# Raw weight blocks behind the mixers on GpSimd's queue, and the residual factors of up behind its third block

## The chip, the cores and the metric

The kernel runs on one core of a Trainium2 chip. The metric is device time in microseconds (us) of one execution. The core's engines work side by side, each through its own instruction list in order: TensorE (PE, with its weight loads as PEld), VectorE (DVE), ScalarE (ACT), GpSimd (POOL) and SyncE (SP). Data moves between memory and the core by transfers that an engine issues into its queue; an instruction that waits for a semaphore holds up everything behind it on that engine.

## The reference

One inference step of a decoder layer, for 512 prompt tokens and 8 decode tokens (520 columns), width 2048, in float32:

```python
y, new = mixer(rmsnorm(x, w['g_mix']), ...)        # RG-LRU and mLSTM heads, w_in and w_out
x = x + y
x = x + cross_attn(rmsnorm(x, w['g_xattn']), mk, mv, w)   # w_mk, w_mv, w_cq, w_co, 4 heads, 256 memory tokens
hf = rmsnorm(x, w['g_ffn'])
x = x + jnp.square(jax.nn.relu(hf @ w['w_up'])) @ w['w_down']   # 2048 -> 8192 -> 2048
```

A final norm follows. `w_mk`, `w_out`, `w_cq`, `w_mv` and `w_co` are 2048 x 2048 each, `w_up` and `w_down` four times that.

## The kernel before, in words

The first 600 us project the input (`w_in`) and run the mixers. Everything after that, "behind the mixers", is built by `rest()` as one list of jobs: half of the keys (`w_mk`), the output projection ("out"), the other half of the keys, the queries ("cq"), the values (`w_mv`) with the attention between them, "co", "up" with 32 units, and four groups of "down" (`d0` to `d3`) with 8 units each.

A large product is done by a Strassen-like scheme (`strassen`): a unit is a 2 x 2 arrangement of weight blocks, made into seven products of 24 matmuls each; in the middle of up a unit takes about 20 us. Each float32 matrix is split into a rounded part and a rest. For a weight block ScalarE casts the rounded part `whi` and VectorE subtracts to get `wlo` (`split_weights`, L98), so each block costs a cast of 1.05 us and a subtraction of 1.22 us. Some of the seven products need sums of raw blocks, made by VectorE at L821.

Raw weight blocks of 512 KB are fetched by `fetch` (L869), the line in question is L876. They land in seven rotating buffers (`raw`, sums too are `raws`), or, at the joints between down groups, in a stage buffer (`rawp`). `load` issues on SP's queue and `store` on GpSimd's; both are the same kind of transfer. Fetches stand some four to seven products ahead of their use and a load must wait until its buffer was read for the last time.

The other operand is a set of seven precomputed operand blocks (`op`), spilled to memory by `spill` (L832, on GpSimd: `tdup`, `tdd0` to `tdd3`, ...) and read back by `batch_load` (L845, on SP), then cast by ScalarE (L846) and subtracted by VectorE (L841). The last block of a set goes from the chip directly (`set_tail`, L861). For the keys, `mem_load` (L1143) reads four operand tiles `op<-dmem`; the first time it does so on GpSimd.

A scheduler with a cost model orders the instructions of each engine behind the mixers, with priorities for fetches and evacuations. The order on an engine is fixed when the kernel is built.

`scale_back` is a task that steps along with the jobs. It forms two factors (inverses by Ln and Exp on ScalarE, each with a table load, L1292 and L1293, and VectorE steps L1294, L1295, L1306, L1309), then reads eight residual blocks (`x<-dx`, L1315), multiplies them (L1319) and stores them on GpSimd (L1320), for use as the starting values of down (`down_load`, L1339). Before, it is started when up begins and lets 16 steps go by first. In up, `up_evac` (L1322) squares the output of a unit (L1329, L1330) and spills it. Down stores its sums by L1347 on GpSimd.

Of the kernel before, what the change touches and what calls it, by code (L numbers as in the profile page):

```python
# [11 lines left out]
AF = mybir.ActivationFunctionType  # L12
# [5 lines left out]
P = 128  # L18
TP = 512
NB = 8  # L20
T = TP + NB
# [24 lines left out]
def tile_trunk(ctx: ExitStack, tc: tile.TileContext, a, o):  # L46
    nc = tc.nc
    V, S, PE, G = nc.vector, nc.scalar, nc.tensor, nc.gpsimd
# [16 lines left out]
    def nm(s):  # L65
        uid[0] += 1
        return f"{s}_{uid[0]}"
# [22 lines left out]
    load = nc.sync.dma_start  # L90
    store = G.dma_start
# [26 lines left out]
    def start(gen, rate=None):  # L118

        tasks.append([gen, rate, 0.0])  # L120
# [152 lines left out]
    scl = keep.tile([P, T], F32, name="scl")  # L273
# [12 lines left out]
    st = {}  # L286
# [498 lines left out]
    def rest():  # L785
# [12 lines left out]
        def enter(name, **pools):  # L798
            def go():
                if "stack" in stage:  # L800
                    stage["stack"].close()
                stage.clear()
                stage["stack"] = ExitStack()
                for n, bufs in pools.items():
                    stage[n] = pool(name + n, bufs, stage["stack"])
            return go

        def tl(tag, shape, dt=F32):
            return stage[tag].tile(list(shape), dt, tag=tag, name=nm(tag))
# [13 lines left out]
        def mixed(b, t):  # L823

            sub(b[:, 0:2], t[:, 1:3], t[:, 0:2])
            sub(b[:, 2], t[:, 2], b[:, 0])
            sub(b[:, 3], t[:, 3], b[:, 2])

        def spill(key, k, wa, wb=None):
            d = td[key][k // 4][:, :, k % 4]  # L830
            if wb is None:
                store(d, wa)  # L832
            else:
                store(d[:, 0:4], wa)
                store(d[:, 4:8], wb)
# [29 lines left out]
        seq, sources, raws, ws = [], [], {}, {}  # L865
# [3 lines left out]
        def fetch(k, q):  # L869
            if k not in seconds:  # L870
                t = praw.tile([P, 8, P], F32, tag="raw", name=nm("raw"))
            else:
                n = "y" if "y" in stage else "x"
                t = stage[n].tile([P, YROW] if n == "y" else [P, 2 * T], F32, tag=n, name=nm("rawp"))
                t = t[:, 0:1024].rearrange("p (a b) -> p a b", b=P)
            load(t, sources[k][q])  # L876
            raws[k, q] = t

        def prep(n):
# [71 lines left out]
        def blocks(box, p):  # L951

            if p == 0:
                box["t"] = tl("t", (P, 4, HT))
            t, out = box["t"], box["out"]
            i = (0, 2, 1, 0, 2, 1, 3)[p]
            if p in (3, 4, 5):
                V.tensor_tensor(out=t[:, i], in0=out, in1=t[:, i], op=ALU.add)
            else:
                S.copy(t[:, i], out)  # L960
            return t
# [53 lines left out]
        def mean_of(v):  # L1015
            for c, ps in zip(HALF, st["ps"]):
                V.scalar_tensor_tensor(out=v[:, c], in0=ps, scalar=1.0 / D, in1=esc[:, c],
                                       op0=ALU.mult, op1=ALU.add)
# [63 lines left out]
        def attn_decode(h):  # L1082
# [23 lines left out]

            q = rows_split(512, dqd[h], None)
            cur = [fetch(b, a["K"]) for b in range(2)]
            for b in range(NB):
                yield  # L1110
                kt, qb = cur.pop(0), spread(q, b, 512)
                for i in range(2):
                    t = kt[:, i * 512:(i + 1) * 512]
                    V.tensor_tensor_reduce(out=t, in0=t, in1=qb, op0=ALU.mult, op1=ALU.add,
                                           scale=1.0, scalar=0.0, accum_out=sc[:, i, b:b + 1])
                if b + 2 < NB:
                    cur.append(fetch(b + 2, a["K"]))
            cur = [fetch(b, a["V"]) for b in range(2)]
            for _ in range(2):
                yield  # L1120
# [46 lines left out]
        def mv_job(h, g, w):  # L1167
            if g == 0:
                st["mv"] = [pacc.tile([P, 512], F32, tag="acc" + b, name=nm("mv")) for b in "bc"]
            wh, wl = (flat(t).rearrange("p (a b) -> p a b", a=2) for t in w)  # L1170
            for j in range(2):
                k = 2 * g + j
                xh, xl = mact[k]
                for i in range(2):
                    ms = slice(i * P, (i + 1) * P)
                    for wi, (x, u) in enumerate(((xh, wh), (xh, wl), (xl, wh))):
                        PE.matmul(st["mv"][i], x[:, ms], u[:, j], start=(k == 0 and wi == 0),  # L1177
                                  stop=(k == KB - 1 and wi == 2))
# [3 lines left out]
        def mv_post(h, g):  # L1182
            if g == 7:
                while h > 1 and not pv_done[h - 2]:
                    step_tasks()
                t = tl("kv", (P, 4 * HT))[:, 0:1024].rearrange("p (a b) -> p a b", a=2)
                for i in range(2):
                    S.activation(t[:, i], st["mv"][i], AF.Copy, scale=rmc[:, i:i + 1])
                    load(o["mv"][h, i], t[:, i])
                mvx[h] = hi, lo = op_tile((P, 2, 512)), op_tile((P, 2, 512))  # L1190
                S.copy(hi, t)
                lo_of(lo, t, hi)
# [92 lines left out]

        def up_enter():
            enter("d", x=2, r=1, t=2, w=2)()
            start(scale_back())

        def negative_inverse(y, t, v):  # L1290

            S.activation(y, v, AF.Ln)  # L1292
            S.activation(y, y, AF.Exp, scale=-1.0)  # L1293
            V.tensor_tensor(out=t, in0=v, in1=y, op=ALU.mult)  # L1294
            V.scalar_tensor_tensor(out=y, in0=t, scalar=2.0, in1=y, op0=ALU.subtract, op1=ALU.mult)  # L1295

        def scale_back():
            for _ in range(16):
                yield

            va, vb = tl("x", (P, 2, T)), tl("x", (P, 2, T))
            v, y, t = va[:, 0], va[:, 1], vb[:, 0]
            mean_of(v)
            st["rphi"] = tl("r", (P, T))
            negative_inverse(y, t, scl)
            V.scalar_tensor_tensor(out=st["rphi"], in0=y, scalar=-1.0, in1=v, op0=ALU.mult, op1=ALU.mult)  # L1306
            yield
            negative_inverse(y, t, v)
            V.scalar_tensor_tensor(out=scl, in0=y, scalar=-1.0, in1=scl, op0=ALU.mult, op1=ALU.mult)  # L1309
            yield  # L1310
            for u in range(KB // 2):
                for _ in range(6):
                    yield
                x = tl("x", (P, 2, T))
                load(x, dx[2][u])  # L1315
                for _ in range(6):
                    yield
                for i in range(2):
                    V.tensor_tensor(out=x[:, i], in0=x[:, i], in1=st["rphi"], op=ALU.mult)  # L1319
                store(dx[3][u], x)  # L1320

        def up_evac(u, p, box):  # L1322
            t = blocks(box, p)
            if u == UP - 1 and p == 0:
                box["w"] = tl("w", (P, 8, HT))
                enter("e", y=4, x=4)()
            if p == 6:
                w = box.pop("w", None) or tl("w", (P, 8, HT))
                S.activation(t, t, AF.Relu)  # L1329
                S.activation(w[:, 0:4], t, AF.Square)  # L1330
                mixed(w[:, 4:8], w[:, 0:4])
                spill(f"d{u // 8}", u % 8, w)

# [94 lines left out]
        for h in range(4):  # L1428
            plain([a["w_mv"][h, g] for g in range(8)],
                  lambda g, w, h=h: mv_job(h, g, w), lambda g, h=h: mv_post(h, g))  # L1430
        seq[first]["enter"] = att_enter
        seq[-1]["after"] = att_left
        strassen("co", 8, sq_src("w_co"), enter_=enter("c", x=2, w=2, sq=1, ss=1),
                 **residual(1, 2, C_FFN, "up"))
        strassen("up", UP, sq_src("w_up"), up_evac, up_enter, lambda s: set_load("d0", s),
                 hooks={(UP - 1, 3): lambda: (down_load(0), down_load(1))})

# [94 lines left out]
def _pack(i):  # L1532
# [58 lines left out]
    y=(KB, P, T), p_m=(4, 1), s_m=(4, NB), scv=(P, 2, 16, NB), cv=(16, P, 11), rh=(8, P, 9),  # L1591
# [39 lines left out]
```

## Time and profile before

| what | value |
| --- | --- |
| runs of the kernel | 2802.77 us median of 3 (2799.02 to 2803.41) |
| profiled execution | 2807.62 us, span 2805.8 us |
| mean granted TensorE clock | 0.977 |
| TensorE busy | 2689.8 us, 21122 matmuls |
| VectorE busy | 2263.9 us |
| ScalarE busy | 1389.2 us |
| GpSimd busy | 106.9 us |
| moved by transfers | 551.23 MB |

A row of a timeline gives the start from the span's begin, the length, the engine, the source line, the operation, output and inputs, the count, and in brackets the idle time before it with what ended that. A row of waits gives total, times and longest in us. Issues of transfers count for SP's queue as SPq, where the time of a row may hold its wait. A row of transfers gives count, size and median us from issue to landing. The profiled execution is 4.85 us above the median of the runs.

### The profile page before, as it was taken

What the parts mean: (1) busy time and instruction counts of PE and PEld (TensorE: products, weight loads), DVE (VectorE), ACT (ScalarE), POOL (GpSimd) and SP (SyncE); (2) the same over time, 40 slices, a digit from 0 to 9 for tenths busy, and PEclk for the clock granted to TensorE, in tenths of its full rate; (3) what the DMA queues carried; (4) which work ended last, traced back from release to release, by engine and by line L of the source; (5) the groups of instructions that cost most, each with busy time, mean ns of one, the idle gap of its engine ahead of it and who ended that gap; (6) DMA issues with size and microseconds to landing.
All of it is one profiled execution on the core that took longest, in us unless ns stands there. A gap on an engine that the chain in (4) does not pass through costs nothing.

```text
span 2805.8 us, 52010 instructions
## 1 busy us (share of the span) xinstructions
PE 2689.8 (96%) x21122; PEld 2612.2 (93%) x21122; DVE 2263.9 (81%) x3453; ACT 1389.2 (50%) x1857; POOL 106.9 (4%) x162
## 2 busy tenths in 40 slices
PE   7999999999999999989979999999999999999996
PEld 7999999999999997669969999999998999999996
DVE  7777787758888888889888777777788787988886
ACT  5455556525455445455464545554554353544543
POOL 0000000030000000000000000000000000000000
PEclk9999999999999999999989999999999999999998
DMA  4666642378677458885657454545457465564632
GB/s 168 191 214 212 198 144 90 104 273 272 217 247 270 158 188 296 314 328 179 220 198 255 148 170 145 173 144 172 146 191 277 146 237 180 207 209 153 234 110 80
DMA packets 178855, 551.23 MB, mean 196 GB/s; under 512 B 23724, under 2 KB 33644, under 8 KB 178616
## 3 DMA queue, kind: packets, MB, share of 16 engines
q1 hardware_dynamic: 153384, 455.28, 48.8%
q0 software_dynamic: 24080, 90.50, 8.9%
q8 instruction: 166, 2.72, 0.4%
q10 hardware_dynamic: 1152, 2.13, 0.2%
q14 instruction: 73, 0.60, 0.1%
HBM read 427.45 MB, written 120.51 MB: 195 GB/s over the span
## 4 chain that ended last, share of the span: by engine, by line
PE 80%; DMA 8%; DVE 6%; ACT 3%; issue 2%; SPq 0%; DVEq 0%; ACTq 0%
PE acca L942 33%; PE accc L942 16%; PE mm L166 12%; PE accb L942 9%; PE mv L1177 3%; PE mk L1157 2%; DVE wlo L102 1%; PE ax L185 1%; DMA op<-tdd 1%; PE row L1104 1%; DVE op L841 1%; PE aux L185 1%; ACT whi L101 1%; DMA ct<-in_C 1%; ACT op L846 1%
## 5 line engine op out<-in xcount | busy, mean ns | idle before, releaser
L942 PE MATMUL acca<-op,whi 128*128 128x260 f32 x5632 | 1042.8, 285 | 30.7 <-ACT t L960 11.9
L942 PEld LDWEIGHTS acca<-op,whi 128*128 128x128 f32 x5632 | 877.6, 190 | 35.6 <-ACT t L960 12.9
L942 PE MATMUL acca<-op,wlo 128*128 128x260 f32 x2816 | 802.7, 285 | 4.3 <-DVE wlo L102 4.2
L101 ACT CAST whi<-raw 128x1024 fp32r<-128x1024 f32 x388 | 406.8, 1050 | 441.9 <-PE acca L942 142.7
L942 PEld LDWEIGHTS acca<-op,wlo 128*128 128x128 f32 x2816 | 536.2, 190 | 6.3 <-DVE wlo L102 6.3
L102 DVE TENSOR_TENSOR wlo<-raw,whi 128x1024 fp32r<-128x1024 f32 x388 | 473.0, 1220 | 64.6 <-ACT whi L101 61.0
L942 PE MATMUL accc<-op,whi 128*128 128x260 f32 x2816 | 515.3, 282 | 1.4 <-DVE op L841 0.9
L101 ACT CAST whi<-raws 128x1024 fp32r<-128x1024 f32 x264 | 277.0, 1049 | 385.8 <-PE accc L942 111.5
L166 PE MATMUL mm<-xa,whi 128*128 128x260 f32 x2624 | 432.9, 287 | 14.2 <-ACT whi L101 8.9
L942 PEld LDWEIGHTS accc<-op,whi 128*128 128x128 f32 x2816 | 434.6, 188 | 3.8 <-issue 1.5
L102 DVE TENSOR_TENSOR wlo<-raws,whi 128x1024 fp32r<-128x1024 f32 x264 | 322.7, 1222 | 119.7 <-ACT whi L101 119.0
L942 PE MATMUL accc<-op,wlo 128*128 128x260 f32 x1408 | 397.2, 282 | 0.0
L166 PEld LDWEIGHTS mm<-xa,whi 128*128 128x128 f32 x2624 | 366.5, 191 | 16.1 <-ACT whi L101 8.9
L166 PE MATMUL mm<-xa,wlo 128*128 128x260 f32 x1312 | 268.8, 286 | 0.0
L942 PE MATMUL accb<-op,whi 128*128 128x260 f32 x1408 | 260.8, 285 | 8.1 <-ACT op L846 4.6
L942 PEld LDWEIGHTS accc<-op,wlo 128*128 128x128 f32 x1408 | 265.3, 188 | 0.0
L942 PEld LDWEIGHTS accb<-op,whi 128*128 128x128 f32 x1408 | 218.9, 190 | 9.5 <-ACT op L846 4.8
L166 PEld LDWEIGHTS mm<-xa,wlo 128*128 128x128 f32 x1312 | 204.2, 190 | 0.5 <-DVE wlo L102 0.3
L942 PE MATMUL accb<-op,wlo 128*128 128x260 f32 x704 | 199.3, 283 | 0.0
L841 DVE TENSOR_TENSOR op<-op,op 128x1040 fp32r<-128x1040 f32 (+3 forms) x136 | 159.9, 1179 | 37.6 <-ACT op L846 26.7
L846 ACT CAST op<-op 128x1040 fp32r<-128x1040 f32 (+1 forms) x112 | 112.2, 1006 | 96.6 <-DMA op<-tdd 51.3
L101 ACT CAST whi<-wraw 128x1024 fp32r<-128x1024 f32 x82 | 85.6, 1044 | 140.3 <-PE mm L166 116.7
(374 smaller groups left out, 3313.1 us busy)
## 6 DMA issues: line engine op xcount, KB each, us to landing
raw<-in_w_up SPq DMA_DIRECT2D x128, 512.0 KB, 3.4
raw<-in_w_down SPq DMA_DIRECT2D x100, 512.0 KB, 3.9
wraw<-in_w_in SPq DMA_DIRECT2D x80, 512.0 KB, 4.1
tdd<-w POOLq DMA_DIRECT2D x32, 1040.0 KB, 6.3
x<-dx SPq DMA_DIRECT2D x56, 520.0 KB, 4.8
op<-tdd SPq DMA_DIRECT2D x56, 520.0 KB, 6.7
dx<-x POOLq DMA_DIRECT2D x48, 520.0 KB, 4.8
raw<-in_w_mk SPq DMA_DIRECT2D x32, 512.0 KB, 5.6
```

The source lines that it names most:

```text
L101: S.copy(hi, raw)
L102: V.tensor_tensor(out=lo, in0=raw, in1=hi.bitcast(F32), op=ALU.subtract)
L166: PE.matmul(ps[:, hf, 0:HT], w[:, j, :], x[:, HALF[hf]], start=(k == 0 and wi == 0), stop=(k == n - 1 and wi == 2))
L185: PE.matmul(out, u, v, start=first and i == 0, stop=last and i == 2)
L841: V.tensor_tensor(out=lo, in0=src, in1=hi.bitcast(F32), op=ALU.subtract)
L846: S.copy(hi[:, 0:n], lo[:, 0:n].bitcast(F32))
L942: PE.matmul(out, u[:, k], x[:, j], start=(new and k == 0 and i == 0), stop=(k == 7 and i == 2), skip_group_check=not new)
L1104: PE.matmul(ps, identr[0:NB, b:b + 1].to_broadcast([NB, P]), r, start=i == 0, stop=i == 1)
L1157: PE.matmul(st["mk"], u[:, i, :], x, start=(k == 0 and wi == 0), stop=(k == KB - 1 and wi == 2))
L1177: PE.matmul(st["mv"][i], x[:, ms], u[:, j], start=(k == 0 and wi == 0), stop=(k == KB - 1 and wi == 2))
```

## The change

Every raw weight block behind the mixers is issued on GpSimd's queue instead of SP's: 416 loads of 512 KB (32 each for `w_mk`, `w_out`, `w_cq`, `w_mv`, `w_co`, 128 each for up and down). `scale_back` is started in the evacuation of unit 2 of up, its first Ln is ordered behind the Square of that evacuation (`mark`), and the mean is taken after the first inverse.

```diff
@@ fetch
-            load(t, sources[k][q])
+            store(t, sources[k][q])
@@ up_enter
-            start(scale_back())
@@ scale_back
-            for _ in range(16):
-                yield
...
-            mean_of(v)
             st["rphi"] = tl("r", (P, T))
-            negative_inverse(y, t, scl)
+            with tc.issue_after(st["mark"].ins):
+                negative_inverse(y, t, scl)
+            mean_of(v)
...
@@ up_evac
-                S.activation(w[:, 0:4], t, AF.Square)
+                ins = S.activation(w[:, 0:4], t, AF.Square)
+                if u == 2:
+                    st["mark"] = ins
+                    start(scale_back())
```

Since the scheduler works on the whole list, some instructions of VectorE and ScalarE change places too, most by a few rows.

GpSimd's list at the begin of the keys. Names are tile and source with running numbers; `tdout` rows are spills of the mixers' output. Before:

```order
L733 DMA tdout_1_114<-hh_489_3210 128x260
L734 DMA tdout_1_114<-kv_1017_7204 128x2x260
L1143 DMA op_1030_7482<-dmem_161 128x1024
L1143 DMA op_1032_7487<-dmem_161 128x1024
L1143 DMA op_1034_7492<-dmem_161 128x1024
L1143 DMA op_1036_7497<-dmem_161 128x1024
L982 DMA dx1_0_137<-x_1142_8142 128x1040
```

After:

```order
L734 DMA tdout_1_114<-kv_1017_7204 128x2x260
...
L876 DMA raw_1073_7632<-in_w_mk 128x1024
L876 DMA raw_1077_7663<-in_w_mk 128x1024
L876 DMA raw_1081_7697<-in_w_mk 128x1024
L876 DMA raw_1085_7728<-in_w_mk 128x1024
L1143 DMA op_1030_7482<-dmem_161 128x1024
L1143 DMA op_1032_7487<-dmem_161 128x1024
L1143 DMA op_1034_7492<-dmem_161 128x1024
L1143 DMA op_1036_7497<-dmem_161 128x1024
L876 DMA raw_1089_7762<-in_w_mk 128x1024
```

Ten raw loads now stand between the last spill and the four operand loads of the keys; the eighth to the tenth wait for the buffers of the first to the third.

SP's list where up begins, with raw loads among the reads of up's operand sets. Before:

```order
L845 DMA op_2293_16296<-tdup_1_120 128x780
L876 DMA raw_2331_16546<-in_w_up 128x1024
L845 DMA op_2299_16334<-tdup_0_119 128x1040
L845 DMA op_2301_16339<-tdup_1_120 128x780
L876 DMA raw_2337_16607<-in_w_up 128x1024
L845 DMA op_2305_16373<-tdup_0_119 128x1040
L845 DMA op_2307_16378<-tdup_1_120 128x780
L845 DMA op_2311_16412<-tdup_0_119 128x1040
L876 DMA raw_2349_16736<-in_w_up 128x1024
L845 DMA op_2313_16417<-tdup_1_120 128x780
L845 DMA op_2320_16464<-tdup_0_119 128x1040
L845 DMA op_2322_16469<-tdup_1_120 128x780
```

After:

```order
L845 DMA op_2293_16296<-tdup_1_120 128x780
L845 DMA op_2299_16334<-tdup_0_119 128x1040
L845 DMA op_2301_16339<-tdup_1_120 128x780
L845 DMA op_2305_16373<-tdup_0_119 128x1040
L845 DMA op_2307_16378<-tdup_1_120 128x780
L845 DMA op_2311_16412<-tdup_0_119 128x1040
L845 DMA op_2313_16417<-tdup_1_120 128x780
L845 DMA op_2320_16464<-tdup_0_119 128x1040
L845 DMA op_2322_16469<-tdup_1_120 128x780
```

The three raw loads are gone from between them, and the operand loads follow each other directly.

GpSimd's list at the end of the third down group, where the fourth takes its first blocks through stage buffers. After (before, these `raw` and `rawp` loads were on SP, `rawp_3740` right behind the last operand loads of that group's successor):

```order
L1348 DMA dx3_5_158<-x_3664_28620 128x1040
L876 DMA raw_3743_29270<-in_w_down 128x1024
L876 DMA raw_3744_29272<-in_w_down 128x1024
L876 DMA raw_3765_29420<-in_w_down 128x1024
L1348 DMA dx3_6_159<-x_3689_28846 128x1040
L1348 DMA dx3_7_160<-x_3690_28848 128x1040
L876 DMA rawp_3740_29238<-in_w_down 128x1024
L876 DMA rawp_3751_29314<-in_w_down 128x1024
```

`rawp_3740` now stands behind the last two residual stores of the group.

More of the change, by code (lines that the diff above doesn't have):

```diff
@@ L1297, in scale_back @@
         def scale_back():
-            for _ in range(16):
-                yield
             va, vb = tl("x", (P, 2, T)), tl("x", (P, 2, T))
             v, y, t = va[:, 0], va[:, 1], vb[:, 0]
+            st["rphi"] = tl("r", (P, T))
+            with tc.issue_after(st["mark"].ins):
+                negative_inverse(y, t, scl)
             mean_of(v)
-            st["rphi"] = tl("r", (P, T))
-            negative_inverse(y, t, scl)
             V.scalar_tensor_tensor(out=st["rphi"], in0=y, scalar=-1.0, in1=v, op0=ALU.mult, op1=ALU.mult)
```

## The prediction

> **What bounds the kernel now.** I read the page's busy times and queue shares first, then the windows by stage, then what SP's queue waits for, and last the timelines at the places where TensorE stands still.
>
> ```profile
> span 2805.8 us, 52010 instructions
> PE 2689.8 (96%) x21122; PEld 2612.2 (93%) x21122; DVE 2263.9 (81%) x3453; ACT 1389.2 (50%) x1857; POOL 106.9 (4%) x162
> ...
> q1 hardware_dynamic: 153384, 455.28, 48.8%
> q0 software_dynamic: 24080, 90.50, 8.9%
> ```
>
> TensorE is busy for 96% of the span, so at most 2805.8 - 2689.8 = 116 us could be had from any cover or reordering. The queue rows give time per byte: GpSimd's queue (software_dynamic) took 0.089 x 16 x 2805.8 / 90.50 = 44 us of one DMA engine per MB, SP's 0.488 x 16 x 2805.8 / 455.28 = 48. A byte is no dearer from GpSimd's queue.
>
> The windows by stage show where the idle time lies (columns: window, length, busy PE, PEld, DVE, ACT, POOL with counts, granted TensorE clock, DMA share, GB/s):
>
> ```profile
> 615.00:630.00 15.00, 10.88 (x74) 10.59 (x74) 10.05 (x13) 7.13 (x8) 0.00 (x0) 0.77 0.86 317
> 1254.00:1270.00 16.00, 7.32 (x39) 5.87 (x38) 15.73 (x22) 12.06 (x25) 0.00 (x0) 0.85 0.68 264
> 1427.00:1466.00 39.00, 19.48 (x116) 18.27 (x117) 34.37 (x44) 26.82 (x37) 0.56 (x1) 0.74 0.55 205
> 1600.00:2080.00 480.00, 480.00 (x4001) 480.00 (x4001) 371.90 (x405) 247.41 (x311) 20.34 (x24) 1.00 0.48 157
> ```
>
> In the middle of up TensorE never stops: nothing can be gained there, only lost. The change decides at stage entries: keys (615), co (1254), co to up (1427), and the four down groups.
>
> **The change, part one: 416 raw loads from SP's queue to GpSimd's.**
>
> ```profile
> SPq L876 <- DVE raws L821: 541.8, 103, 11.9
> SPq L876 <- DVE wlo L102: 353.1, 140, 12.7
> ...
> raw<-in_w_up SPq DMA_DIRECT2D x128, 512.0 KB, 3.4
> ...
> dx<-x POOLq DMA_DIRECT2D x48, 520.0 KB, 4.8
> ...
> L832 POOL DMA_DIRECT2D tdd<-w x32 | 27.2, 850 | 582.1 <-DVE w L821 501.6 <-ACT whi L101 36.7 <-DVE wlo L102 19.9
> L1143 POOL DMA_DIRECT2D op<-dmem x4 | 2.2, 546 | 15.3 <-DMA tdout<-hh 13.5 <-PE mm L166 1.8
> ```
>
> L876 is the raw load: SP stands for hundreds of us at it, until VectorE frees one of seven buffers. It issues in order, so an operand load (L845) behind it stands too. That is the cost the move can take away. Its own cost: one issue of 512 KB on GpSimd took 546 ns (L1143), so 416 x 0.546 = 227 us on an engine busy for 107 us: hidden. Landing goes from 3.4 us towards 4.8 (520 KB stores); the steady stage covers that:
>
> ```profile
> 1685.53 6.64 SPq L876 DMA_DIRECT2D raw<-in_w_up  x2
> 1693.32 1.23 DVE L821 TENSOR_TENSOR raws<-raw,raw 128x1024 f32<-128x1024 f32 x1
> ```
>
> The load issued at 1685.53 has its first use at 1693.32, the tightest of a unit: 7.8 us against 4.8. Queued behind it is a second raw load and then the spill `tdd<-w`; in the new order of GpSimd the raws stand in the sequence in which these were issued in time, so none waits for a later one. Steady units: 0.
>
> VectorE could be slowed by GpSimd's issues, or GpSimd by VectorE. The 0.85 us above are means over 32 issues made while VectorE was 77% busy (371.90 of 480), so 227 us more of such issues cost nothing visible; bounds 0 to a few us. The Trainium skill (SBUF — State Buffer, section SBUF: two separate sides) says that GpSimd cannot write descriptors while VectorE runs an operation that takes both ports, and advises loads on SP or ACT instead, against this change. The trace shows no such delay at 850 and 546 ns; by its figure of some 3.1 us for such a DMA instead of 0.62, an estimate from that page, each raw load would be 2.5 us later, still inside the 7.8.
>
> **Where it loses: the keys.** Four operand loads `op<-dmem` (L1143) already sit on GpSimd. In the new order ten raw loads stand ahead of them, the tenth waiting for VectorE's third `wlo`:
>
> ```profile
> 597.25 0.57 POOL L1143 DMA_DIRECT2D op<-dmem  x1
> 615.62 1.22 DVE L102 TENSOR_TENSOR wlo<-raw,whi 128x1024 fp32r<-128x1024 f32 x1
> 615.96 1.03 ACT L1144 CAST op<-op 128x1024 fp32r<-128x1024 f32 x1
> 617.04 0.79 PE L1157 MATMUL mk<-op,whi 128*128 128x256 f32 x2 [2.41 <-ACT op L1144]
> 619.91 0.58 PE L1157 MATMUL mk<-op,whi 128*128 128x256 f32 x1 [2.08 <-DVE op L841]
> ...
> op<-dmem POOLq DMA_DIRECT2D x4, 512.0 KB, 7.6
> ```
>
> That `wlo` ends at 616.84; the tenth raw load issues, then the four: first at 617.4. Landing 7.6 gives 625.0, the cast 1.03 more: TensorE begins at about 626 instead of 617.04. The second stall (2.08) then falls inside the first, so the loss is 9 - 2 = 7. The key jobs are bound by TensorE and make none of it up; later waits of the same stage (some 2 us before the next product) absorb a part. I take +5; bounds +2 (landing of 4.8) and +10 (nothing absorbed).
>
> **Where it gains: co to up.**
>
> ```profile
> 1445.83 0.33 SPq L876 DMA_DIRECT2D raw<-in_w_up  x1
> 1455.59 0.33 SPq L876 DMA_DIRECT2D raw<-in_w_up  x1
> 1456.01 1.33 SPq L845 DMA_DIRECT2D op<-tdup  x3
> 1465.18 0.96 DVE L841 TENSOR_TENSOR op<-op,op 128x780 fp32r<-128x780 f32 x1
> 1445.04 0.58 PE L942 MATMUL accb<-op,whi 128*128 128x260 f32 x1 [4.59 <-ACT op L846]
> 1463.34 0.80 PE L942 MATMUL acca<-op,whi 128*128 128x260 f32 x2 [10.05 <-ACT t L960]
> 1475.78 0.51 PE L942 MATMUL acca<-op,whi 128*128 128x260 f32 x2 [1.61 <-DVE t L958]
> ```
>
> SP stands at a raw load until 1445.83 and at the next until 1455.59, and the last three operand loads go at once behind it, at 1456, with nothing else in the trace that held them. TensorE loses 4.59 + 10.05 + 1.61 = 16.3 us. What is late next is VectorE: of the 39 us to 1466 it was busy for 34.4, so at most 4.6 us of idle close up in its part, and the moved residual work (below), three VectorE steps of 0.7, takes 2.1 us out of the stretch. The last `lo` ends 6.7 us earlier. The 1.61 at 1475.78 and the clock (0.74 in this window, since it follows the stalls) give a little more. I take -10; bounds -4 (VectorE's idle time alone) and -16 (all of TensorE's three waits).
>
> The same mechanism is smaller elsewhere. At the entry of co VectorE was busy for 15.73 of 16 us, so -1.5 (0 to -3). At the down groups:
>
> ```profile
> 2292.93 0.32 SPq L1339 DMA_DIRECT2D x<-dx  x1
> 2293.34 0.38 SPq L845 DMA_DIRECT2D op<-tdd  x1
> 2299.88 0.80 PE L942 MATMUL acca<-op,whi 128*128 128x260 f32 x2 [3.18 <-ACT whi L101]
> 2131.37 0.51 PE L942 MATMUL acca<-op,whi 128*128 128x260 f32 x2 [1.37 <-ACT whi L101]
> 2608.85 9.80 SPq L876 DMA_DIRECT2D rawp<-in_w_down  x3
> 2615.10 0.53 POOL L1347 DMA_DIRECT2D dx<-x  x1 [2.26 <-DVE x L949]
> 2619.45 0.39 PE L942 MATMUL acca<-op,wlo 128*128 128x260 f32 x1 [1.75 <-DVE wlo L102]
> ```
>
> At 2293 an operand load stood behind a residual load; in the new order it stands ahead of it, and the 3.18 goes: -4 with the slow clock after it (0 to -4). At the first group, 2131, the load behind residuals and raws came late: -2 (0 to -3). At the last group it turns round: the first `rawp` (a raw load into another buffer), issued at 2608.85 on SP, now stands behind both last residual stores of the group, so after 2615.6, 6.8 us later, and its cast, at 2614.7 before, moves to about 2620: +3 (0 to +5).
>
> **Part two: the residual factors.**
>
> ```profile
> 1436.57 1.28 ACT L1292 ACT_TABLE_LOAD   x1
> 1437.87 0.64 ACT L1292 ACTIVATE x<-scl 128x520 f32<-128x520 f32 x1
> 1468.24 0.70 DVE L1294 TENSOR_TENSOR x<-x 128x520 f32<-128x520 f32 x1 [2.09 <-ACT x L1293]
> ```
>
> Four table loads of 1.28 and four activations of 0.64, 7.7 us of ACT, leave co to up for units 2 and 3 of up, with five VectorE steps and sixteen multiplies of about 0.7. ACT is half busy there; VectorE has 0.23 x 20.2 = 4.6 us idle in each unit and the work is spread over seven units: 15 of 32 us. New in it: raws that stand on GpSimd behind residual stores, which wait for multiplies and for `x<-dx` loads. +1 (0 to +4). The gain of leaving was counted above.
>
> **Sum.** +5 - 10 - 1.5 - 4 - 2 + 3 + 1 = -8.5 us on the profiled execution's 2807.6 (span 2805.8 and 1.8 around it), 2799.1. The median of the runs, 2802.8, lies 4.8 below that execution, so the forecast is 2794.3. The ends of the terms add to -24 (2 - 16 - 3 - 4 - 3) and +15 (10 - 4 + 5 + 4), which all together are unlikely.
>
> **Rivals.** *No measurable change:* VectorE gives only its lower bound at co to up (-4), and the keys lose 8: +8 - 4 - 1.5 - 4 - 2 + 3 + 1 = +0.5, 2803. For it: VectorE at 88% in that window; TensorE needs its sets in order, and the last sets wait for VectorE. The Trainium skill (DMA: Bandwidth & Descriptors, Issuing engines are not separate DMA queues) says that issuing from several engines saves only the sequencer's time to issue. By that rule the 0.33 us of an SP issue is all there is to save, off the path, and the time would be about this rival's; the waits of 542 and 353 us in SP's queue speak against it, since these are waits of a queue and not bandwidth.
>
> *Larger gain:* the loads in advance let TensorE run through co to up (-16) while the keys lose only 2 and the last group nothing: 2 - 16 - 1.5 - 4 - 2 + 0 + 0 = -21.5, 2781.
>
> *Slower, through the tight raw load of every unit:* if a load on GpSimd's queue lands more than 7.8 us after its turn, each of 64 units of up and down waits for the excess. The four `op<-dmem` took 7.6, in a stretch with the DMA engines 86% busy; the stores of 520 KB took 4.8, and the steady stage has them 48% busy, so it is near the point only at the entries. At 1 us of excess: +64 - 8.5 = +55, 2858.
>
> **How the numbers follow.** Runs of this kernel agree to about 0.2% (5.6 us). My forecast case 0.5, no change 0.23, larger gain 0.14, slower units 0.08, the rest (a wider loss at keys, a reordering of VectorE that costs) 0.05. The forecast case spreads from 2786 to 2800: 0.40 of it faster, 0.10 same. No change: 0.17 same, 0.03 each way. With the larger gain's 0.14, faster is 0.57, same 0.27, slower 0.03 + 0.08 + 0.05 = 0.16. The range goes from 2781 to 2809: the larger gain, no change, and a small loss.
>
> **What would show it.** Right: the keys' first matmul near 626; operand loads of up on SP in one run without a raw between, all issued by 1440; the 10 us wait at 1463 gone, and the first unit of up ending near 1464; the wait at 2299.9 gone; steady units at the same length. Wrong: GpSimd's raw loads landing after 7 us in the middle of up, TensorE waits for `whi` or `raws` there, or VectorE operations longer than 1.22 us.

## The result, and the profile after

The changed kernel took 2819.86 us (median of 4 runs, 2817.94 to 2821.23) against 2802.11 for the kernel before: ratio 1.0055, 95% interval 1.0039 to 1.0072. It is slower by some 17.7 us; the forecast was 2794.3 with a range to 2809. The profiled execution has a span of 2819.4 us. Its page:

```profile
span 2819.4 us, 52063 instructions
PE 2689.6 (95%) x21122; PEld 2610.0 (93%) x21122; DVE 2261.6 (80%) x3453; ACT 1387.8 (49%) x1857; POOL 330.5 (12%) x578
...
q0 software_dynamic: 83984, 308.63, 32.6%
q1 hardware_dynamic: 93480, 237.15, 24.8%
...
raw<-in_w_up POOLq DMA_DIRECT2D x128, 512.0 KB, 4.4
raw<-in_w_down POOLq DMA_DIRECT2D x100, 512.0 KB, 4.3
```

The reader sees the bytes move from q1 to q0 and GpSimd's busy time grow by 224 us, as worked out (227). TensorE's and VectorE's work is the same. A raw load of up lands in 4.4 us instead of 3.4. The time is lost in waits.

Where it is lost shows when the two traces are compared matmul by matmul: the kernel after is behind by so much at the same number of matmuls. One trace is one execution, so the kernel before was traced a second time (the first experiment) and both columns stand here, in us of loss (+) or gain (-) over each stretch, by the time of the first trace of before:

| stretch | against the first trace | against the second | the sum's term |
| --- | --- | --- | --- |
| up to 600 (unchanged part) | +1.2 | +3.0 | 0 |
| 600-625, keys begin | +6.5 | +6.4 | +5 |
| 625-700, keys to output product | +2.7 | +5.2 | (in the +5) |
| 870-920, queries begin | +5.0 | +4.6 | none |
| 920-1245, values and attention | +6.9 | +5.3 | none |
| 1245-1300, co begins | +2.2 | +1.5 | -1.5 |
| 1300-1470, co to up | -7.0 | -8.1 | -10 |
| 1470-1530, to the end of unit 2 of up | -6.1 | -6.4 | (in the -10) |
| 1530-1600, units 3 to 6 of up | +7.7 | +7.7 | +1 |
| 1600-2100, the rest of up | +0.4 | +0.4 | 0 |
| 2100-2160, first down group | -2.1 | -2.7 | -2 |
| 2160-2320, second down group | -5.6 | -1.0 | -4 |
| 2480-2640, last down group | +4.4 | +4.7 | +3 |

With the stretches left out (all under 1.5) the columns add to +14.0 and +18.5; the medians differ by 17.7. Not only VectorE's and ScalarE's lists changed places: by shape and names TensorE's own matmuls come in another order too, at 480 places up to 1290 us, 374 of them in the stage of the values (1060 to 1240) and 70 between 670 and 700. There a matmul count compares the two kernels only as a whole, from the stretch's begin to its end.

At the keys, timelines of GpSimd, ScalarE and TensorE in the kernel after:

```profile
618.35 0.53 POOL L876 DMA_DIRECT2D raw<-in_w_mk  x1 [5.29 <-DVE wlo L102]
618.87 2.10 POOL L1143 DMA_DIRECT2D op<-dmem  x4
625.39 1.04 ACT L1144 CAST op<-op 128x1024 fp32r<-128x1024 f32 x1 [8.12 <-DMA op<-dmem]
626.49 0.80 PE L1157 MATMUL mk<-op,whi 128*128 128x256 f32 x2 [10.64 <-ACT op L1144]
627.75 0.58 PE L1157 MATMUL mk<-op,whi 128*128 128x256 f32 x1 [0.46 <-DVE op L841]
```

The tenth raw load waits 5.29 us for `wlo`, the four operand loads go behind it, and the first matmul comes at 626.5 where 617.0 stood, with the second wait gone from 2.08 to 0.46. The forecast was 626, and this execution came 1.2 us late to the place, so this step of the prediction is right within a microsecond.

From co to up, SP's issues and TensorE's waits:

```profile
1433.99 21.75 SPq L845 DMA_DIRECT2D op<-tdup  x14
1466.15 0.39 PE L942 MATMUL acca<-op,whi 128*128 128x260 f32 x1 [2.54 <-DVE op L841]
1479.77 0.80 PE L942 MATMUL acca<-op,whi 128*128 128x260 f32 x2 [5.54 <-ACT t L960]
```

All fourteen operand loads go in one run, which ends at 1455.7 where TensorE is 23 us late: some 1432 by the clock of before, which had its last at 1457. The wait of 10.05 at the place is 5.54, not gone, and those of 4.59 and 2.52 before it are one of 2.54.

In units 3 to 6 of up, SP, GpSimd, VectorE and TensorE, and SP's wait row for 1540 to 1640:

```profile
1554.85 25.72 SPq L1313 DMA_DIRECT2D x<-dx  x5
SPq L1313 <- DMA dx<-x: 49.9, 6, 20.5
1572.06 0.54 POOL L1318 DMA_DIRECT2D dx<-x  x1
1573.62 0.54 POOL L1318 DMA_DIRECT2D dx<-x  x1 [1.02 <-DVE x L1317]
1584.24 0.70 DVE L1317 TENSOR_TENSOR x<-x,r 128x520 f32<-128x520 f32 x1 [7.05 <-DMA x<-dx]
1584.86 1.22 DVE L102 TENSOR_TENSOR wlo<-raws,whi 128x1024 fp32r<-128x1024 f32 x1
1586.13 0.39 PE L942 MATMUL acca<-op,wlo 128*128 128x260 f32 x1 [4.17 <-DVE wlo L102]
```

VectorE stands for 7.05 us in a residual multiply whose load has not landed, with the `wlo` that TensorE needs right behind it. SP issued five residual loads in 25.7 us: there are two buffers (`enter("d", x=2, ...)`), so each load waits until the store of two blocks earlier has landed, which is the wait row `dx<-x`. From the store of block 1 at 1572.06 to the multiply of block 3 at 1584.24 it took 12.2 us.

At the last down group, GpSimd, ScalarE and TensorE:

```profile
2624.67 0.54 POOL L1348 DMA_DIRECT2D dx<-x  x1 [1.73 <-DVE x L949]
2625.20 0.54 POOL L876 DMA_DIRECT2D rawp<-in_w_down  x1
2630.50 1.04 ACT L101 CAST whi<-rawp 128x1024 fp32r<-128x1024 f32 x1 [7.02 <-DMA rawp<-in_w_down]
2631.60 0.80 PE L942 MATMUL acca<-op,whi 128*128 128x260 f32 x2 [4.81 <-ACT whi L101]
```

The raw block goes right behind the second store, and TensorE waits 4.81 for its cast.

### The profile page after: what moved, and what is told of

The parts are those of the page before. It is cut to its first block, busy times and chain, and to the rows that moved or that the text cites. A ratio compares the mean times of both kernels' runs of the same rounds, so it can differ in the third digit from the quotient of the medians.

```text
span 2819.4 us, 52063 instructions
## 1 busy us (share of the span) xinstructions
PE 2689.6 (95%) x21122; PEld 2610.0 (93%) x21122; DVE 2261.6 (80%) x3453; ACT 1387.8 (49%) x1857; POOL 330.5 (12%) x578
## 4 chain that ended last, share of the span: by engine, by line
PE 77%; DMA 8%; DVE 7%; issue 3%; ACT 3%; SPq 0%; POOL 0%; DVEq 0%; ACTq 0%; POOLq 0%
PE acca L942 32%; PE accc L942 16%; PE mm L166 12%; PE accb L942 8%; PE mv L1177 2%; DVE wlo L102 2%; PE ax L185 1%; DMA op<-dmem 1%; DMA op<-dq 1%; PE row L1104 1%; PE mk L1157 1%; ACT whi L101 1%; DVE op L841 1%; PE aux L185 1%; DMA dmk<-sq 1%
## 5 line engine op out<-in xcount | busy, mean ns | idle before, releaser
L942 PE MATMUL acca<-op,whi 128*128 128x260 f32 x5632 | 1040.0, 285 | 35.8 <-ACT whi L101 11.2
L102 DVE TENSOR_TENSOR wlo<-raw,whi 128x1024 fp32r<-128x1024 f32 x388 | 472.6, 1219 | 78.1 <-ACT whi L101 74.0
```

What stands on the lines that cost most here:

```text
L102: V.tensor_tensor(out=lo, in0=raw, in1=hi.bitcast(F32), op=ALU.subtract)
L942: PE.matmul(out, u[:, k], x[:, j], start=(new and k == 0 and i == 0), stop=(k == 7 and i == 2), skip_group_check=not new)
```

## The experiments

The medians below are compared with runs of the kernel before on the same chip; those had medians of 2803.0, 2804.7 and 2807.0 us in the three sets.

**The kernel before, once more.** No edit.

> The kernel before, unchanged, for a second profiled execution: how far two executions of one kernel differ from place to place. Theory A: matmul by matmul the two agree within 2 us at every place from 600 us on, and the ledger of places from single traces stands. Rival B: some of the places (attention, co to up, the joints of the down groups) differ by 3 us or more between two executions, and part of what was put down to the change is chance.

Measured: a span of 2801.3 us. Most places agree within 2 us, but not the second down group, where this execution is 4.6 us faster than the first. The same wait in the second trace:

```profile
2297.78 0.51 PE L942 MATMUL acca<-op,whi 128*128 128x260 f32 x2 [1.15 <-ACT whi L101]
```

It was 3.18. Rival B holds at that place, and 625-700 differs by 2.5; theory A holds elsewhere. The -4 that the prediction took there rested on a wait that the kernel does not always have.

**One part at a time.**

```diff
 # raw loads alone (base: before)
-            load(t, sources[k][q])
+            store(t, sources[k][q])
```

> The raw loads go to GpSimd's queue as in the change, the residual factors stay as in the kernel before. Theory A (each place's loss or gain belongs to the raw loads there, and the one long TensorE wait of 4.2 us near 1586 us in up belongs to the moved residual factors): all the losses up to co stay (TensorE some 23 us behind the kernel before at the end of co), the step from co to up gives back less than the 12 us it gave with the whole change since the four table loads and the VectorE steps lie in it again, say 8, and the 6 us lost near 1586 are not lost: about 2817 us, 15 over before. Rival B (the move of the factors makes no difference, the whole effect is the queue's): 2820. Rival C (the gain from co to up belongs to the factors): nothing given back there, about 2826.

Measured: 2825.8 us, ratio 1.0077 (1.0056 to 1.0098), 9 above theory A's 2817. From 1420 to 1530 this kernel gains only 2.1 us, where the whole change gains 12.8, and it loses 2.1 instead of 7.7 from 1530 to 1600. So the long wait near 1586 does belong to the moved factors, as theory A had it. The rest shows when the stretch is cut at 1470. Up to there, where the operand sets are loaded and split, the raw loads alone gain 4.4 of the 6.6 us of the whole change. From 1470 to 1530, in the first units of up, the whole change gains 6.1 and the raw loads alone lose 2.3. There the residual multiplies stand where they stood before. VectorE, kernel before (the first two rows, one multiply and its wait row for 1460 to 1700) and this kernel:

```profile
1502.45 0.70 DVE L1319 TENSOR_TENSOR x<-x,r 128x520 f32<-128x520 f32 x1 [3.82 <-DMA x<-dx]
DVE x L1319 <- DMA x<-dx: 9.3, 6, 3.8
1552.39 0.70 DVE L1319 TENSOR_TENSOR x<-x,r 128x520 f32<-128x520 f32 x1 [6.71 <-DMA x<-dx]
DVE x L1319 <- DMA x<-dx: 14.5, 4, 6.7
```

So VectorE stood in the multiplies for residual loads before the change as well, 9.3 us in all, and longer with the raw loads moved.

```diff
 # factors alone (base: after)
-            store(t, sources[k][q])
+            load(t, sources[k][q])
```

> The residual factors stand behind block 2 of up as in the change, all raw loads stay on SP's queue. Theory A: no loss before up; from co to up the 7.7 us of ScalarE and 2 us of VectorE that left give some 3 us; the wait near 1586 for the multiply of residuals stays and costs 5: about 2804 us, +2 on before. Rival B (factors make no difference): 2802. Rival C (the gain from co to up is theirs): 12 us gained there, 2795 or less.

Measured: 2804.3 us, ratio 0.9998 (0.9984 to 1.0013). From 1420 to 1530 it gains 7.2, from 1530 to 1600 it loses 9.2. Of the 7.2 only 1.0 lie up to 1470, at the operand sets; 6.1 lie from 1470 to 1530, as many as with the whole change, and all raw loads are on SP here. The place where the operand sets load is thus mostly the raw loads' (4.4 and 1.0 alone, 6.6 together). The rest is the residual work leaving the first units of up, and the 9.2 are the price of the same work in units 3 to 6, where VectorE's waits for residual loads are 9.7 us (10.0 in the whole change): moved, not removed. The total is as theory A said, since gain and loss of the second part cancel.

**The keys put back.** The first four groups of sources are the first half of `w_mk`.

```diff
-            store(t, sources[k][q])
+            (store if k >= 4 else load)(t, sources[k][q])
```

> The changed kernel with only the first half of the keys' weights (16 raw loads, the first four groups) back on SP's queue, so that the four op<-dmem loads stand again right behind the last spill on GpSimd. Theory A (the in-order queue holds these four loads behind the tenth raw load): the first matmul of the keys is back near 617 us, and the 6.6 us lost there, with the 3 us lost by the time of the output product, return: about 2811 us. Rival B (the queue of GpSimd is slower at this place whatever stands ahead): the first matmul stays near 626, 2820. Rival C (the later stages absorb it): the keys start at 617, but the total stays within 3 us of 2820.

Measured: 2816.2 us, ratio 1.0041 (1.0027 to 1.0055). The trace has the four operand loads and the first matmul where the kernel before has them:

```profile
595.00 0.57 POOL L1143 DMA_DIRECT2D op<-dmem  x1
611.96 0.53 POOL L1143 DMA_DIRECT2D op<-dmem  x1 [0.90 <-PE mm L166]
614.78 0.80 PE L1157 MATMUL mk<-op,whi 128*128 128x256 f32 x2 [2.41 <-ACT op L1144]
```

(This execution was 2.3 us ahead before that place.) The 6.5 us are not lost, -0.1 instead. The order of GpSimd's list is the cause, rival B falls. The 3 us between 650 and 700 stay, so they come from another part, perhaps the loads of the output product: all the traces that lose 2.5 or more there have these on GpSimd, and TensorE's matmuls in another order with it. These loads alone were not tried. The total came between theory A's 2811 and rival C's 2820: some 4 us returned by the two ratios, whose intervals overlap.

**The values put back too.** Sources 24 to 31 are `w_mv`.

```diff
+            (load if k < 4 or 24 <= k < 32 else store)(t, sources[k][q])
```

> The changed kernel with the raw loads of the first half of the keys and of the values (w_mv, the stage of the attention) back on SP's queue, all others on GpSimd's. Theory A (the 8 to 10 us lost between 1055 and 1250 us belong to the value loads on GpSimd): TensorE is about level with the kernel before at 1250 instead of 11 behind, and the time is some 2807, 9 under the kernel that has only the keys back. Rival B (they belong to the order that SP's other loads take in that stage once raw loads leave SP elsewhere): no change there, 2816.

Measured: 2800.2 us, ratio 0.9985 (0.9972 to 0.9997). Against the kernel that has only the keys back the ratio went from 1.0041 to 0.9985, some 15 us, 10 to 21 by the intervals: the largest single share of the loss, and more than theory A's 9. In the traces TensorE loses 9.8 us from 1055 to 1245 with the values on GpSimd (keys back), and 2.4 from 1055 to 1200 with them back on SP; this trace has another 6.2 at 1200-1245, so it is 10.6 behind at 1250 and does not show theory A's level there. The spaced kernel below, with the same order of every engine's instructions up to 1545 us, loses nothing in the stage (-0.9). Over all traces, the three with all value loads and their neighbours on GpSimd lose 6.5 to 10.6 from 1055 to 1245; of the ten with the value loads on SP all but this one lie between -0.9 and 3.5.

**The values alone on GpSimd** (base: before).

```diff
+            (store if 24 <= k < 32 else load)(t, sources[k][q])
```

> The kernel before with the 32 value loads (w_mv) alone on GpSimd's queue. Theory A (these loads cost the attention stage some 10 to 16 us): about 2815, +12 on before. Rival B (the stage loses only when other loads of the neighbouring stages moved too, since the planner orders SP's list otherwise): 2804, no difference.

Measured: 2810.5 us, ratio 1.0013 (1.0000 to 1.0026), a loss of 0 to 7 us: less than theory A, more than rival B. So some 4 us belong to these loads by themselves; the other 10 or so came only with more loads moved, though between 1060 and 1240 TensorE, VectorE and ScalarE have the same order here as with only the keys back. Why is open. Waits in the stage show where the time goes. ScalarE and SP in the kernel before, 1062 to 1245, then the kernel after, 1078 to 1266, there with a row of TensorE's waits:

```profile
ACT op L1201 <- DMA op<-dq: 7.0, 3, 3.0
ACT op L1201 <- DMA op<-dmk: 6.5, 2, 4.0
ACT rowh L1092 <- DMA rowl<-dqd: 1.4, 1, 1.4
SPq L1098 <- DVE od L1133: 32.0, 14, 6.1
```

```profile
ACT op L1201 <- DMA op<-dq: 11.9, 6, 4.8
ACT op L1201 <- DMA op<-dmk: 3.0, 2, 1.7
ACT rowh L1092 <- DMA rowl<-dqd: 5.0, 2, 4.3
SPq L1098 <- DVE od L1133: 44.6, 14, 9.7
PE ax L185 <- ACT op L1201: 5.1, 3, 3.3
```

ScalarE stands longer for the reads of query operands (`op<-dq`) and rows (`rowl<-dqd`), which stay on SP, and less for `op<-dmk`: 19.9 us for the three instead of 14.9. TensorE stands for ScalarE (5.1 us, the last row; before, it has no wait of this kind in the stage). What makes these waits longer was not told apart. The transfer engines were no busier (0.84 of the stretch, 0.86 before), which speaks against the raw blocks taking turns with the reads there. SP stands longer at its loads of keys and values for VectorE (`kv`, L1098: 131 us in all its rows, 103 before), and the reads stand behind these in its list. And wherever the value loads are on GpSimd the scheduler also put TensorE's matmuls of this stage in another order, which no run tried by itself.

**The multiplies left out.** Raw loads of up and down alone on GpSimd (256), with the multiplies and without.

```diff
+            (store if k >= 40 else load)(t, sources[k][q])
 # and in the second kernel:
-                for i in range(2):
-                    V.tensor_tensor(out=x[:, i], in0=x[:, i], in1=st["rphi"], op=ALU.mult)
```

> The changed kernel with raw loads on GpSimd's queue only for up and down (256 of 416), the earlier stages' loads on SP as before. Theory A (losses at keys, queries, attention and co belong to the raw loads of those stages; gains from co to up and at the second down group to those of up and down): the 23 us lost by the end of co are not lost, the gain of 12 from co to up stays, as do the loss of 6 near 1586 and of 4.5 at the last down group and the gains of 9 at the first three groups: about 2791 us, 11 under before. Rival B (the gain from co to up is only lateness given back, since loads that were late relative to TensorE are no longer late when TensorE itself is 23 us behind): nothing gained there, about 2803.

> Raw loads of up and down on GpSimd's queue, and the sixteen multiplies of the residual by the factor left out (the residual is loaded and stored unscaled), to see what they cost. Theory A (VectorE's in-order wait in them): TensorE's wait near 1580 us goes, 8 us between 1530 and 1600 return, about 2795 us against 2803 with the multiplies. Rival B (the wait comes from the raw loads that stand behind the residual stores on GpSimd's queue): the wait stays at 4 us or more, 2802.

Measured: with them 2803.2 us, ratio 1.0002 (0.9989 to 1.0015); without, 2795.7, ratio 0.9964 (0.9952 to 0.9977). In the trace of the first the gain from co to up is 13.5 us from 1420 to 1530, so rival B of that run, lateness given back, falls: it is there when TensorE is not late at all. It was eaten up by 8.6 us between 1530 and 1600 and 4.7 at the last group, as theory A listed, but the 9 at the down groups which it counted too are 5.8 against the first trace and 1.5 against the second, so in large part the chance of the first. Without the multiplies TensorE loses 2.7 from 1530 to 1600, its longest wait there is 1.5, and by the ratios some 10 us of time return:

```profile
PE accc L942 <- DVE wlo L102: 1.5, 1, 1.5
```

So the multiplies make most of the wait (5.9 of the 8.6 us), not the raw loads on GpSimd; with every raw load on SP it is there too (9.2 above). The kernel without the multiplies leaves out the scaling of the residual and only serves to measure this.

**The multiplies on GpSimd**, with the raw loads of the first four units of up alone on its queue.

```diff
+            (store if 40 <= k < 44 else load)(t, sources[k][q])
-                    V.tensor_tensor(out=x[:, i], in0=x[:, i], in1=st["rphi"], op=ALU.mult)
+                    G.tensor_tensor(out=x[:, i], in0=x[:, i], in1=st["rphi"], op=ALU.mult)
```

> Raw loads on GpSimd's queue for the first four units of up alone (16 of 416), and the sixteen multiplies of the residual by the factor done by GpSimd in place of VectorE; the factors stand behind block 2 as in the change. Theory A (VectorE, which works in order, stood in the multiply for a residual load that waits for a store two blocks earlier, and TensorE behind it): the 8 us between 1530 and 1600 are not lost, the gain of some 13 from co to up stays, nothing is lost at the last down group: TensorE ends 12 to 14 ahead, about 2791 us. Rival B (the wait moves to GpSimd's queue, and the raw loads behind the multiply come late): a wait of TensorE for whi near 1580 as long as the old one, about 2800. Rival C (the gain from co to up needs all raw loads of up and co away from SP): less than 6 gained there, about 2798.

Measured: 2803.9 us, ratio 0.9994 (0.9981 to 1.0006). The gain from co to up is there in full (12.7 from 1420 to 1530), so 16 loads moved do for that as well as 256, and rival C falls. But 11.2 us are lost from 1530 to 1600, for a reason that no theory had. Timelines of VectorE and GpSimd:

```profile
1537.68 1.80 DVE L102 TENSOR_TENSOR wlo<-raws,whi 128x1024 fp32r<-128x1024 f32 x1 [1.12 <-ACT whi L101]
1539.40 1.81 DVE L821 TENSOR_TENSOR w<-w 128x520 f32<-128x520 f32 x1
1541.13 4.07 DVE L821 TENSOR_TENSOR raws<-raw,raws 128x1024 f32<-128x1024 f32 x1
1537.07 3.58 POOL L1317 TENSOR_TENSOR x<-x,r 128x520 f32<-128x520 f32 x2 [15.75 <-DMA x<-dx]
1541.56 2.56 POOL L1317 TENSOR_TENSOR x<-x,r 128x520 f32<-128x520 f32 x2
```

While GpSimd multiplies, VectorE's operations of 1.22 us take 1.80 and 4.07, and one of 0.69 takes 1.81. On SP raw loads of the later units stand behind residual loads again.

**The multiplies spaced.** Each pair is ordered on VectorE behind the mixing of the latest unit, 1.7 units of up apart. Base: keys and values back on SP.

```diff
-            V.tensor_tensor(
+            return V.tensor_tensor(          # in sub; mixed returns its last sub
-                mixed(w[:, 4:8], w[:, 0:4])
+                st["vmark"] = mixed(w[:, 4:8], w[:, 0:4])
+                with tc.issue_after(st["vmark"].ins):
+                    for i in range(2):
+                        V.tensor_tensor(out=x[:, i], in0=x[:, i], in1=st["rphi"], op=ALU.mult)
```

> The kernel with the first half of the keys and the values back on SP (2800 in its own comparison, 4 under before), and each pair of residual multiplies ordered on VectorE behind the mixing of the latest unit, so that they stand some 1.7 units apart instead of half a unit. Theory A (VectorE stands in a multiply whose load waits for the store of two blocks earlier, because eight blocks follow each other faster than store and load through memory take): TensorE's wait near 1580 goes, 7 of the 8 us between 1530 and 1600 return, about 2793. Rival B (the cost is VectorE's 11 us of multiplies themselves, wherever they stand in up): the loss spreads over the later units, 2800.

> As the spaced kernel, with the raw loads of the last down group (32) also back on SP, so that the first of them no longer stands behind two residual stores. Theory A (that order costs 4.5 us at the last group's begin): about 2789, 4 under the spaced one. Rival B (SP's residual and operand loads hold it as long): no difference.

> All raw loads on SP as before, the factors behind block 2 and their multiplies spaced: what the second part is worth with its flaw mended and without the first. Theory A: 5 to 7 us gained from co to up (the factors' share of it) and nothing lost in up: about 2798, and the raw loads of up and down on GpSimd are worth the further 5 us to the spaced kernel. Rival B (the raw loads' move is worth nothing once the factors are out of the way): same as the spaced kernel.

Measured: spaced 2794.9 us, ratio 0.9957 (0.9940 to 0.9973); with the last down group's loads back as well 2791.6, ratio 0.9943 (0.9927 to 0.9958); spaced with every raw load on SP 2797.3, ratio 0.9965 (0.9952 to 0.9978). In all three, 1530 to 1600 costs 0.9 us instead of 8. The waits of TensorE from 1500 to 1620 in the second of them:

```profile
PE acca L942 <- ACT x L1292: 0.7, 1, 0.7
```

Theory A is shown: it was how close the multiplies stood, not their work, for that is all still there, and in none of the three does a multiply wait for a residual load any more. With its loads back on SP the last group loses nothing (-0.1 us) instead of 4.7 (theory A), but the intervals of the first two overlap. The third shows what the first part is worth beside the second: co to up gains 8.5 us from 1420 to 1530 with all raw loads on SP, and 13.6 with up's on GpSimd, a difference of 5 there, all of it before 1470; in the total the intervals overlap, so rival B is not excluded. The second kernel, some 15 us faster than before and, by the two ratios, 31 faster than the changed one, is the best version found.

## Why the prediction was wrong

Most of the signs that the prediction named came true: the keys at 626, the operand loads in one run, the wait at 2299.9 gone, steady units unchanged; only the 10 us wait was halved and not gone. The time was wrong all the same, because none of the signs lay in the stages of the queries, values and attention or in the residual multiplies.

**The keys (+5).** Right in place and mechanism, and the size at the place (6.5) within its bounds. The step that failed is "later waits absorb a part": nothing came back, and the next 75 us lost 3 to 5 more, not because of these four loads.

**Co to up (-10).** The -13 to -15 lie between the bounds partly by luck. At the place itself, up to 1470, the change gained 7 to 8, and the raw loads have most of it, as forecast (4.4 to 5), the factors 1.0 to 2.4 (forecast 2.1). The other 6.1 lie in the first units of up and come whenever the residual work leaves them. The prediction counted 2.1 us of VectorE's work for the leaving and not its waits for residual loads; the 1.61 that it showed at 1475.78 was a part of that wait, since VectorE's `t` (L958) stands right behind multiplies that waited 1.62 us for their load.

**The factors in up (+1, at most +4).** Mis-sized: 7.7 here, 9.2 alone. The prediction compared VectorE's work with VectorE's idle time (15 of 32 us) and found it covered. What counts in an in-order list is when the inputs arrive. The multiplies stood half a unit apart; a store, a load into the buffer it frees, and the next multiply took 12 us. It named the waits "for multiplies and for `x<-dx` loads" but hung them on the raw loads of GpSimd's queue, where they did no harm, and not on the `wlo` behind the multiply. The same wait was in the kernel before, in the first units, so moving the work could not cover it; spacing did.

**Queries, values and attention (no term).** The step that failed is one that is missing. The stages were named as moved (160 of 416 loads) and not looked at for what the move does to the rest: ScalarE waits longer for the reads that stay on SP (19.9 us instead of 14.9), and TensorE's order changed. It cost 15 us by the two ratios, more than any term of the sum; by which of these ways stays open. The entry of the queries, 5.0 here and 6.2 with the raw loads alone, is not settled: the spaced kernel and the one with its last group back, with the same order there, lost 4.5 and 1.2.

**The entry of co (-1.5).** It did not come: +2.2 and +1.5 in the table, and 0.6 to 2.4 against the first trace in every other one, on whichever queue co's loads are. No gain or loss of the change is shown there.

**Down groups.** The last one (+3) was 4.4 to 4.7, and 4.2 to 4.9 in all seven traces with its loads on GpSimd, against -0.3 to 2.9 in the others. The first (-2) was 2.1 to 2.7, but other kernels range from -2.9 to 0.5 with the loads on GpSimd and from -1.8 to 0.6 with them on SP, so no gain is shown (these and the next against the first trace). The second (-4) was read from a wait that a second execution of the same kernel has at 1.15 instead of 3.18. All eight traces with its loads on GpSimd are 5.4 to 5.8 ahead of the first trace there, and the six with them on SP 0 to 4.7, 2.8 in the mean; so a gain of some 3 is real.

**The rest.** Steady units are the same (0.4 us in 500), raw loads land in 4.4 us inside the 7.8, and VectorE's `wlo` took 1219 ns against 1220 with 224 us more of issues on GpSimd, each of which took 0.53 to 0.54 us in the mean. The Trainium skill (SBUF — State Buffer, section SBUF: two separate sides) describes that GpSimd's transfers wait while VectorE runs an operation that takes both ports. Such a delay did not show here. The slower rival, built on late raw loads in each unit, did not happen.

## What to carry to other kernels

When loads go to another engine's queue, look at each stage for what stood in that queue already and now stands behind them, for what stays in the old queue, and for what the scheduler orders otherwise because of the move; at co to up, 16 loads moved gained as much as all 416. Work that moves under a half-busy engine is covered only if its inputs are there when its turn comes: measure the round trip of its buffers (12 us here), and space it by that. A term read from one wait of one execution is worth a second trace of the kernel before.

## What the hardware showed

GpSimd computing and VectorE computing slow each other: a VectorE operation of 1.22 us took up to 4.07 beside GpSimd's multiplies, which took 1631 ns in the mean, against 1276 for five multiplies of the same shape on GpSimd at the end of that trace (L1386), and 0.70 us on VectorE:

```profile
L1317 POOL TENSOR_TENSOR x<-x,r 128x520 f32<-128x520 f32 x16 | 25.7, 1631 | 26.6 <-DMA x<-dx 26.6
```

GpSimd issuing transfers does not: 416 more issues left VectorE's `wlo` at 1219 ns (1220 before). Executions with the same order of instructions up to a place differ there by 4 us or more (4.6 at a down group, 3.7 at the queries' begin, 9 in the attention), and the medians of before alone ranged from 2802.1 to 2807.0 between sets.
